# A decoder layer on one core: the up projection as seven half-size block products

## The chip, the cores and the metric

The kernel runs on one core of a Trainium2 chip. The metric is the device time of one execution in microseconds (us). The kernel before takes 798.82 us, the median of three runs (798.44 to 799.29).

## The reference

One layer of a hybrid decoder, for one sequence of 512 tokens of width 1024, in float32. The first half mixes tokens (a state-space group and a forgetting-attention group, side by side) and ends in an output projection that is added to the residual. The second half, which the change is about, is a gated MLP with a short convolution:

```python
x = x + (mixed @ w_out[layer].astype(mixed.dtype)).astype(x.dtype)
hf = rms_norm(x, norm_ffn_w[layer])
x = x + conv_gated_mlp(hf, w_up[layer], ffn_conv_w[layer], ffn_conv_b[layer], w_down[layer]).astype(x.dtype)
...
def conv_gated_mlp(x, w_up, conv_w, conv_b, w_down):
    h = x @ w_up.astype(x.dtype)                    # 512 x 1024 by 1024 x 5632
    h = causal_depthwise_conv(h, conv_w, conv_b)    # width 3, along the tokens
    gate, val = jnp.split(h, 2, axis=-1)            # 2816 columns each
    return (jax.nn.silu(gate) * val) @ w_down.astype(x.dtype)
```

## The kernel before, in words

**Arithmetic.** Every large matrix product is made of three matmuls in a reduced float32 format (`mm3`, line 88): each operand is split into a high part, a rounded copy that ScalarE makes, and a low part, the rest, which VectorE subtracts; high x high, high x low and low x high are summed in PSUM. So each block of weights (128 x 1024 numbers, 512 KB) is loaded by a DMA from SyncE's queue into a tile `wraw`, and split into `wh` and `wl` by one operation of ScalarE (line 84) and one of VectorE (line 85); three buffers of each turn round.

**Order.** The program is written in the order of the work, and a scheduler then orders the instructions of each engine beforehand by modelled times and priorities (`urgent()` raises a block's priority); on the chip each engine then takes its instructions in that fixed order. PSUM has eight banks of 128 x 512 numbers: three in the pool `pg`, four in `pm`, one in `po`.

**End of the mixer.** Projections of the attention heads are interleaved with pieces of the output projection (`fillers`, line 670; `a1` is a half of the second state-space group, `o0` to `o2` the first attention groups). The last piece, `out_proj((7,), mf[6:8])` (line 696), goes half of the output columns by half, and within each over the four blocks of 128 tokens. Each result is added to the residual `x2` by VectorE (line 258).

**Into the MLP.** GpSimd multiplies `x2` with the norm's weight (line 709), TensorE transposes the result (`hT`, line 712), and ScalarE and VectorE split it into `hh` and `hl`. The norm itself, a factor for each token, is not applied here: `second_norm` (line 792) sums the squares, takes the power on GpSimd (line 103) and spreads the factors over the partitions with a matmul (`rbc`, line 124) into `R2`.

**Up projection.** For each of 44 tiles of 128 output features `up_proj` (line 773) makes 8 x 3 matmuls of 512 columns (tokens) into one bank; the first tile is cut into two halves of 256 columns, 48 matmuls. `gated(j)` (line 805) multiplies the bank with `R2` (VectorE, line 811), makes the convolution with one operation of ScalarE (line 814) and two of VectorE (line 816), and applies SiLU to the gate (line 821). GpSimd forms gate x value and the sums S1 to S4 that the next step needs (lines 826 to 840).

**Down projection.** It is a block product already made of seven half-size products instead of eight (`PRODUCTS`, line 860), in tiles Y, X and Z. Its weights come in six units for each product; sums of weight blocks are formed in tiles `T` by DMAs of GpSimd's queue that add while they write (`gather`, line 758), after plain loads (`fresh`, line 755). The results are added to `x2` and stored.

Lines of the profile that the prediction uses: 84 and 85 (weight splits), 91 (all `mm3` matmuls), 103 (power on GpSimd), 124 (`rbc`), 258 (residual), 466 (a normalisation with two factors, in the mixer), 618 (a copy out of PSUM), 759 (issue of an adding DMA), 796 (squares), 811 to 829 (`gated`).

Of the kernel before, what the change touches and what calls it, by code (L numbers as in the profile page):

```python
# [8 lines left out]
F32 = mybir.dt.float32  # L9
# [29 lines left out]
def tile_hybrid_layer(  # L39
# [25 lines left out]
    pg = ctx.enter_context(tc.tile_pool(name="pg", bufs=3, space=PSUM))  # L65
    pm = ctx.enter_context(tc.tile_pool(name="pm", bufs=4, space=PSUM))
    po = ctx.enter_context(tc.tile_pool(name="po", bufs=1, space=PSUM))
# [20 lines left out]
    def mm3(o, ah, al, bh, bl, start, stop, grouped=True, keep=False):  # L88
        kw = {} if grouped else {"skip_group_check": True}
        for n, (a, b) in enumerate(((ah, bh), (ah, bl), (al, bh))):  # L90
            ins = pe.matmul(o, a, b, start=start and n == 0, stop=stop and n == 2, **kw)  # L91
            if keep:
                tc.keep_in_program_order(ins)

    def bank(name="g"):
        return pg.tile([P, 512], F32, tag="g", name=name)

    def mbank(name="m"):
        return pm.tile([P, 512], F32, tag="m", name=name)
# [241 lines left out]
    def ssd_proj(g):  # L341
# [6 lines left out]
        def to_tokens(j, src):  # L348
            t = po.tile([P, 512], F32, tag="o", name="xT")
# [255 lines left out]
    def fox_values(pair, turned, v):  # L605
        o = po.tile([P, 512], F32, tag="o", name="o")
# [9 lines left out]
        mh = pf.tile([P, SEQ], F32R, tag="mfh", name="mfh", bufs=2)  # L616
        ml = pf.tile([P, SEQ], F32R, tag="mfl", name="mfl", bufs=2)
# [7 lines left out]
    early = {8: b0, 10: feature_tile(second), 0: feature_tile(third, po.tile([P, 512], F32, tag="o", name="j0"))}  # L625
# [18 lines left out]
    pss_ctx.close()  # L644
    pf_ctx = ExitStack()
# [25 lines left out]

    def fill(name):
        if name[0] == "a":
# [22 lines left out]
    out_proj((7,), mf[6:8])  # L696

    hh = pxt.tile([P, NK, SEQ], F32R, tag="xh", name="hh")
    hl = pxt.tile([P, NK, SEQ], F32R, tag="xl", name="hl")
    nw = pf.tile([P, 1280], F32, tag="prob", name="nw", bufs=4)[:, :D]  # L700
    nc.sync.dma_start(nw, norm_ffn_w.to_broadcast([P, D]))
    for half in range(2):
        c = slice(half * 512, (half + 1) * 512)
        ks = slice(half * 4, half * 4 + 4)
        for tb in range(NTB):
            s = slice(tb * P, (tb + 1) * P)
            with urgent():
                xw = pf.tile([P, 512], F32, tag="pt1" if tb % 2 else "pt2", name="xw", bufs=3)
                (dve if (half, tb) == (1, 3) else pool).tensor_tensor(out=xw, in0=x2[:, tb, c], in1=nw[:, c], op=ALU.mult)
                t = mbank("hT")  # L710
                for j in range(4):
                    pe.transpose(t[:, j * P : (j + 1) * P], xw[:, j * P : (j + 1) * P], ident)
                tv = t.rearrange("p (j f) -> p j f", j=4)
                act.copy(hh[:, ks, s], tv)
                dve.tensor_sub(hl[:, ks, s], tv, raw(hh[:, ks, s]))
    pf_ctx.close()
    actx.close()

    pb = ctx.enter_context(tc.tile_pool(name="pb", bufs=1, reuse_waits="tile"))
    NH = NFF // 2  # L720
    HT = SEQ // 2
    N1, N2 = slice(0, 512), slice(512, 1024)

    def operand(slot=None):
        if slot is None:
            hl_ = [pb.tile([P, NH, HT], F32R, tag=t, name=t, bufs=2) for t in ("oh", "ol")]
            return hl_[0], hl_[1]
        pair_ = [pxt.tile([P, NK, SEQ], F32R, tag=t, name="o" + t) for t in ("xh", "xl")]
        return tuple(
            t.rearrange("p a b -> p (a b)")[:, 0 : NH * HT].rearrange("p (a b) -> p a b", b=HT) for t in pair_  # L730
        )

    a11, a12 = operand(), operand()
    a22 = pb.tile([P, NH, HT], F32, tag="a22", name="a22")
    S1, S2, S3, S4 = [pb.tile([P, NH, HT], F32, tag="S%d" % n, name="sum%d" % n) for n in (1, 2, 3, 4)]
    r2 = pb.tile([P, NTB], F32, tag="r2", name="r2")
    ss = pb.tile([P, NTB], F32, tag="ss", name="ss")
    UNITS = [(k, min(k + 2, NH)) for k in range(0, NH, 2)]
    B11, B12, B21, B22 = 0, 1, 2, 3
# [3 lines left out]

    raws = [0]

    def load_unit(q, u):
        where = wp if raws[0] % 5 < 3 else pb
        raws[0] += 1
        rw = where.tile([P, 1024], F32, tag="wraw", name="wraw", bufs=3 if where is wp else 2)
        nc.sync.dma_start(rw[:, 0 : (UNITS[u][1] - UNITS[u][0]) * 512], part(q, u))  # L750
        return rw
# [8 lines left out]

    def split_unit(u, src):
# [3 lines left out]
        act.copy(h[:, :n], src[:, :n])  # L765
        dve.tensor_tensor(out=l[:, :n], in0=src[:, :n], in1=raw(h[:, :n]), op=ALU.subtract)  # L766
        return h, l

    pu_ctx = ExitStack()
    pu = pu_ctx.enter_context(tc.tile_pool(name="pu", bufs=1, reuse_waits="tile"))  # L770
    R2 = pu.tile([P, SEQ], F32, tag="R2", name="R2")

    def up_proj(fs, cuts, between=None):
        ws = [load_split(wup[f], four=False) for f in fs]
        os = [bank("up") for _ in fs]
        w = SEQ // cuts
        for cut in range(cuts):
            s = slice(cut * w, (cut + 1) * w)
            for o, (h, l) in zip(os, ws):
                for k in range(NK):  # L780
                    ks = slice(k * P, (k + 1) * P)
                    pin = between is not None and k == NK // 2
                    if pin:
                        between()
                    mm3(
                        o[:, s], h[:, ks], l[:, ks], hh[:, k, s], hl[:, k, s], k == 0 and cut == 0, k == NK - 1,
                        grouped=cuts == 1, keep=pin,
                    )
        return os


    def second_norm():
        with urgent():
            for tb in range(NTB):
                junk = pb.tile([P, D], F32, tag="junk", name="junk", bufs=2)
                act.activation(junk, x2[:, tb, :], AF.Square, accum_out=ss[:, tb : tb + 1])
            token_scale(r2, R2, ss, pu)

    early = up_proj((0,), 2) + up_proj((NFF,), 1, between=second_norm)
# [5 lines left out]
    def gated(j):  # L805
        both = []
        for part in range(2):
            f = part * NFF + j
            o = early[part] if j == 0 else up_proj((f,), 1)[0]
            xp = pu.tile([P, SEQ], F32, tag="up", name="up", bufs=3)  # L810
            dve.tensor_mul(xp, o, R2)  # L811
            a = pu.tile([P, SEQ], F32, tag="ua", name="ua", bufs=5)
            cw = C_FCW + 3 * f
            act.activation(a, xp, AF.Identity, scale=pc[:, cw + 2 : cw + 3], bias=pc[:, C_FCB + f : C_FCB + f + 1])
            for s in range(1, 3):
# [210 lines left out]
```

## Time and profile before

| What | Value |
|---|---|
| Median of three runs | 798.82 us |
| Lowest and highest | 798.44 and 799.29 us |
| Span of the profiled execution | 799.4 us |
| TensorE (PE), weight loads (PEld) busy | 791.7, 645.6 us |
| VectorE (DVE), ScalarE (ACT), GpSimd (POOL) busy | 566.8, 428.7, 223.9 us |
| Granted TensorE clock over the span | 0.998 |
| Moved from and to HBM | 91.56 MB read, 2.20 MB written |
| End of the last down product to the end of the span | 794.6 to 799.4 us |

A busy time is the time in which at least one instruction of the engine ran; weight loads run beside matmuls. In a row of a group stand the line of the kernel, the engine, the operation, the tiles (out<-in), the shapes and the count, then busy time in us and mean of one in ns, then the idle time of the engine just before these instructions and what ended it. In a row of the chain or the timeline the first two numbers are start and duration in us. In a row of the windows each engine has its busy time and its count of instructions; the last three numbers are TensorE's clock, the mean busy share of the 16 DMA engines and GB/s.

### The profile page before, as it was taken

What the parts mean: (1) busy time and instruction counts of PE and PEld (TensorE: products, weight loads), DVE (VectorE), ACT (ScalarE), POOL (GpSimd) and SP (SyncE); (2) the same over time, 40 slices, a digit from 0 to 9 for tenths busy, and PEclk for the clock granted to TensorE, in tenths of its full rate; (3) what the DMA queues carried; (4) which work ended last, traced back from release to release, by engine and by line L of the source; (5) the groups of instructions that cost most, each with busy time, mean ns of one, the idle gap of its engine ahead of it and who ended that gap; (6) DMA issues with size and microseconds to landing.
All of it is one profiled execution on the core that took longest, in us unless ns stands there. A gap on an engine that the chain in (4) does not pass through costs nothing.

```text
span 799.4 us, 10603 instructions
## 1 busy us (share of the span) xinstructions
PE 791.7 (99%) x3789; PEld 645.6 (81%) x3789; DVE 566.8 (71%) x891; ACT 428.7 (54%) x779; POOL 223.9 (28%) x260
## 2 busy tenths in 40 slices
PE   8999999999999999999999999999999999999997
PEld 6888887877887877887877888888888888888886
DVE  4797997688567576597874677766766766778744
ACT  6556646552479477775752563444443444556531
POOL 0003231433233362243200434233333223233120
PEclk9999999999999999999999999999999999999999
DMA  9524322431244234252231463223223223299992
GB/s 325 179 80 138 130 80 80 146 131 53 80 159 132 54 130 133 68 161 89 84 100 54 134 183 106 92 92 106 93 91 106 98 87 106 91 247 190 219 189 91
DMA packets 31254, 98.12 MB, mean 123 GB/s; under 512 B 3873, under 2 KB 4961, under 8 KB 31201
## 3 DMA queue, kind: packets, MB, share of 16 engines
q1 hardware_dynamic: 26192, 81.71, 30.6%
q0 software_dynamic: 4576, 15.21, 10.1%
q8 instruction: 30, 0.49, 0.2%
q10 hardware_dynamic: 432, 0.52, 0.2%
q14 instruction: 24, 0.19, 0.1%
HBM read 91.56 MB, written 2.20 MB: 117 GB/s over the span
## 4 chain that ended last, share of the span: by engine, by line
PE 98%; DMA 1%; DVE 0%; SPq 0%; ACT 0%; DVEq 0%; issue 0%
PE up L91 30%; PE pw L91 22%; PE po L91 11%; PE g L91 7%; PE Y L91 5%; PE X L91 4%; PE Z L91 4%; PE o L610 2%; PE pT L600 2%; PE yd L436 2%; PE j L91 1%; PE S L577 1%; PE S L578 1%; PE qkT L527 1%; PE yo L442 1%; DMA xr<-in_xT_dram 1%
## 5 line engine op out<-in xcount | busy, mean ns | idle before, releaser
L84 ACT CAST wh<-wraw 128x1024 fp32r<-128x1024 f32 x103 | 108.1, 1050 | 109.0 <-PE up L91 75.2
L85 DVE TENSOR_TENSOR wl<-wraw,wh 128x1024 fp32r<-128x1024 f32 x103 | 132.0, 1282 | 26.2 <-ACT wh L84 23.9
L91 PE MATMUL up<-hh,wh 128*128 128x512 f32 (+1 forms) x360 | 138.9, 386 | 0.0
L91 PE MATMUL up<-hh,wl 128*128 128x512 f32 (+1 forms) x360 | 138.5, 385 | 0.0
L91 PE MATMUL up<-hl,wh 128*128 128x512 f32 (+1 forms) x360 | 138.5, 385 | 0.0
L91 PE MATMUL pw<-wh,xh 128*128 128x512 f32 x256 | 102.5, 402 | 0.0
L91 PE MATMUL pw<-wl,xh 128*128 128x512 f32 x256 | 101.8, 398 | 0.0
L91 PE MATMUL pw<-wh,xl 128*128 128x512 f32 x256 | 101.2, 397 | 0.0
L91 PEld LDWEIGHTS up<-hh,wh 128*128 128x128 f32 x360 | 67.6, 188 | 13.7 <-issue 0.2
L91 PEld LDWEIGHTS up<-hl,wh 128*128 128x128 f32 x360 | 67.6, 188 | 13.6 <-issue 0.2
L91 PEld LDWEIGHTS up<-hh,wl 128*128 128x128 f32 x360 | 67.6, 188 | 13.3
L811 DVE TENSOR_TENSOR up<-up,R 128x512 f32<-128x512 f32 x44 | 30.3, 691 | 58.6 <-PE up L91 58.6
L816 DVE SCALAR_TENSOR_TENSOR ua<-up,pc,ua 128x511 f32<-128x511 f32 (+1 forms) x88 | 66.8, 763 | 1.3
L91 PEld LDWEIGHTS pw<-wh,xl 128*128 128x128 f32 x256 | 48.1, 188 | 9.9 <-issue 0.5
L91 PEld LDWEIGHTS pw<-wl,xh 128*128 128x128 f32 x256 | 48.2, 188 | 9.6 <-issue 0.7
L91 PEld LDWEIGHTS pw<-wh,xh 128*128 128x128 f32 x256 | 48.1, 188 | 9.5 <-issue 0.5
L765 ACT CAST wh<-T 128x1024 fp32r<-128x1024 f32 (+1 forms) x30 | 29.3, 976 | 36.9 <-PE Z L91 15.3
L579 DVE CUSTOM_DVE_ANT_0 prob<-S,prob 128x128 f32<-128x128 f32 (+1 forms) x64 | 30.3, 487 | 24.7 <-PE S L578 24.4
L766 DVE TENSOR_TENSOR wl<-T,wh 128x1024 fp32r<-128x1024 f32 (+1 forms) x30 | 33.8, 1134 | 19.2 <-ACT wh L765 18.8
L583 ACT ACTIVATE prob<-prob,nm 128x128 f32<-128x128 f32 (+1 forms) x64 | 35.8, 560 | 21.1 <-DVE nm L579 20.4
L258 DVE TENSOR_TENSOR x<-po,x 128x512 f32<-128x512 f32 x48 | 32.6, 686 | 13.1 <-PE po L91 12.9
L826 POOL TENSOR_TENSOR ua<-ua 128x512 f32<-128x512 f32 x11 | 15.0, 1363 | 91.0 <-DVE ua L816 91.0
(238 smaller groups left out, 1691.9 us busy)
## 6 DMA issues: line engine op xcount, KB each, us to landing
wraw<-in_wup_dram SPq DMA_DIRECT2D x44, 512.0 KB, 3.3
T<-in_wdown_dram POOLq DMA_DIRECT2D x20, 512.0 KB, 7.1
wraw<-in_wqk_dram SPq DMA_DIRECT2D x16, 512.0 KB, 3.3
wraw<-in_wout_dram SPq DMA_DIRECT2D x16, 512.0 KB, 3.3
wraw<-in_wxbc_dram SPq DMA_DIRECT2D x11, 512.0 KB, 6.2
wraw<-in_wdown_dram SPq DMA_DIRECT2D x10, 512.0 KB, 3.6
T<-in_wdown_dram SPq DMA_DIRECT2D x10, 512.0 KB, 5.3
wraw<-in_wz_dram SPq DMA_DIRECT2D x8, 512.0 KB, 3.3
```

Source lines behind the costliest of these rows:

```text
L84: act.copy(h, r)
L85: dve.tensor_tensor(out=l, in0=r, in1=raw(h), op=ALU.subtract)
L91: ins = pe.matmul(o, a, b, start=start and n == 0, stop=stop and n == 2, **kw)
L258: dve.tensor_add(dst, banks[tb], dst)
L436: pe.matmul(yd[:, h * HD : (h + 1) * HD], sc[:, h, :], xdt[:, h * HD : (h + 1) * HD], start=True, stop=True)
L579: dve.tensor_tensor_reduce(out=p, in0=sps[:, :n], in1=p, scale=-1.0, scalar=-NEG, op0=ALU.add, op1=ALU.min, accum_out=nm[:, qb : qb + 1],)
L583: act.activation(p, p, AF.Exp, scale=-1.0, bias=nm[:, qb : qb + 1], accum_out=sm[:, qb : qb + 1])
L600: pe.transpose(t[:, w : w + P], prob[:, o : o + P], ident)
L765: act.copy(h[:, :n], src[:, :n])
L766: dve.tensor_tensor(out=l[:, :n], in0=src[:, :n], in1=raw(h[:, :n]), op=ALU.subtract)
L811: dve.tensor_mul(xp, o, R2)
L816: dve.scalar_tensor_tensor(out=a[:, s:], in0=xp[:, : SEQ - s], scalar=pc[:, cw + 2 - s : cw + 3 - s], in1=a[:, s:], op0=ALU.mult, op1=ALU.add,
```

## The change

**Up projection.** The normalised input is cut into four blocks A (two halves of the tokens by two halves of the 1024 inner features), the weights into four blocks B (two halves of the inner features; gate and value columns). For each `q` of 11 the gate and value features of tiles `q` and `q + 11`, four output tiles, are made by seven products of one A-operand with one weight block (128 x 1024) each. A product is 2 tiles x 4 inner pieces x 3 matmuls of 256 columns. The operands are A11, A12, A22, S1 = A21 - A22, S2 = S1 - A11, A11 - A21 and A12 + S2, made once and split; the weight operands are B11, B21, B22 and the sums B11 + B12, B11 + B12 + B22, B11 + B12 + B21 + B22 and B22 + B12. These sums grow in place in the tiles `ta` and `tb`, by adding DMAs from GpSimd's queue after each split. Each group owns two pairs of banks, G and Z; a product that is used in several results is accumulated on in the same half of a bank, and what is needed in between is copied out by ScalarE (`keep`, three times) or joined in PSUM by VectorE (three times). Two groups fill all eight banks.

**Norm.** The norm of each block of 128 tokens is now applied to `x2` before the transposes (`up_tokens`), so `rbc` and the multiplication with `R2` go; the convolution reads PSUM directly.

**Output projection.** Its end goes token block by token block (`out_part`): for each block the rest of `a1` (blocks 2 and 3), then both halves of the last group, then `up_tokens` of that block; the last block's transposes stand behind one and a half products of the up projection. The first three units of the first down product stand among the last products of the up projection, and the order of splits is held by hand (`ordered`). Below, `n2`, `n3` and `n5` are left out: they have the form of `n0` and `n1`, each with a split of `ta` or `tb`, an adding DMA and a product into a half of Z or G; `low12` subtracts a kept half from Z.

```diff
+    for tb in range(NTB):
+        if tb > 1:
+            out_part(wa1[0], m1, 1, (tb,))
+        for half in range(2):
+            out_part(w7[half], mf[6:8], half, (tb,))
+        if tb < NTB - 1:
+            with urgent():
+                up_tokens(tb)
...
+    def up_tokens(tb):
+        half, i = tb // 2, tb % 2
+        xw = xws[half][:, i, :]
+        s = slice(i * P, (i + 1) * P)
+        act.activation(xw, x2[:, tb, :], AF.Square, accum_out=ss[:, tb : tb + 1])
+        rt = r2[:, tb : tb + 1]
+        rsqrt(rt, ss[:, tb : tb + 1], 1.0 / D, 1)
+        t = two_banks("Z", "hT")
+        for c in range(2):
+            cs = slice(c * 512, (c + 1) * 512)
+            dve.scalar_tensor_tensor(
+                out=xw[:, cs], in0=x2[:, tb, cs], scalar=rt, in1=nw[c], op0=ALU.mult, op1=ALU.mult
+            )
+            for j in range(4):
+                o = c * 512 + j * P
+                pe.transpose(t[:, c, j * P : (j + 1) * P], xw[:, o : o + P], ident)
...
+        if half == 0:
+            act.copy(oh[:, 0:2, :, s], tv)
+            dve.tensor_sub(ol[:, 0:2, :, s], tv, raw(oh[:, 0:2, :, s]))
+            act.copy(one[:, :, :, s], tv)
+        else:
+            act.copy(two[:, 1, :, s], tv[:, 1])
+            dve.tensor_sub(s1[:, :, s], tv[:, 0], two[:, 1, :, s])
+            h = act.copy(oh[:, 3, :, s], s1[:, :, s])
+            l = dve.tensor_sub(ol[:, 3, :, s], s1[:, :, s], raw(oh[:, 3, :, s]))
...
+    def split_up(r):
+        h = wp.tile([P, 1024], F32R, tag="wh", name="wh", bufs=3)
+        l = wp.tile([P, 1024], F32R, tag="wl", name="wl", bufs=3)
+        ordered(act.copy(h, r), lambda: dve.tensor_tensor(out=l, in0=r, in1=raw(h), op=SUB))
+        return h, l
...
+    def product(w, n, o, part, first=False):
+        h, l = w
+        ah, al = up_operand(n)
+        for p in range(2):
+            for k in range(4):
+                c = slice(p * 512 + k * P, p * 512 + (k + 1) * P)
+                ins = mm3(
+                    o[:, p, part], h[:, c], l[:, c], ah[:, k], al[:, k], first and k == 0, k == 3, grouped=False
+                )
...
+    def keep(src, name):
+        t = pu.tile([P, 2, HT], F32, tag="kept", name=name, bufs=4)
+        take(act.copy(t, src))
+        return t
...
+    def more(t, quarter, q):
+        last_more[0] = nc.gpsimd.dma_start(t, wup[quarter, q], accum_op=ALU.add)
+
+    def n0(q):
+        u = quads[q]
+        u.ta = ptt.tile([P, 1024], F32, tag="T", name="Ta", bufs=2)
+        nc.sync.dma_start(u.ta, wup[B11, q])
+        w = split_up(u.ta)
+        more(u.ta, B12, q)
+        u.G = two_banks("G", "G")
+        product(w, 0, u.G, H2, True)
+        with urgent():
+            u.y0 = keep(u.G[:, :, H2], "y0")
+
+    def n1(q):
+        u = quads[q]
+        r = wp.tile([P, 1024], F32, tag="wraw", name="wraw", bufs=3)
+        nc.sync.dma_start(r, wup[B21, q])
+        product(split_up(r), 1, u.G, H1)
+        with urgent():
+            take(None, dve.tensor_tensor(out=u.G[:, :, H1], in0=u.G[:, :, H1], in1=u.y0, op=ADD))
...
+    def n6(q):
+        u = quads[q]
+        product(split_up(u.tb), 5, u.G, H2)
+        with urgent():
+            take(None, dve.tensor_tensor(out=u.Z[:, :, H2], in0=u.z2, in1=u.G[:, :, H2], op=SUB))
+
+    def n4(q):
+        u = quads[q]
+        product(split_up(u.ta), 2, u.G, H2)
...
+    for q in range(2, NH - 2):
+        n0(q + 1)
+        n6(q)
+        n2(q + 1)
+        n4(q)
+        gated(q)
+        n1(q + 1)
+        n5(q + 1)
+        n3(q + 1)
+        low12(q + 1)
```

More of the change, by code (lines that the diff above doesn't have):

```diff
@@ L1 @@
[L1 removed]
+from contextlib import ExitStack, nullcontext
 import concourse.bass as bass
@@ new lines, in take @@
+    def take(on_act, on_dve=None):
+        taken[made[0] - 1] = (on_act, on_dve)
+    class Quad:
+        pass
+    quads = [Quad() for _ in range(NH)]
+    H1, H2 = slice(0, HT), slice(HT, SEQ)
+    halfway = [None]
+    def product(w, n, o, part, first=False):
[7 more added lines that the diff above has]
+                )
+            if p == 0:
+                halfway[0] = ins
@@ new lines, in n3, with n5, low12 @@
+    def n3(q):
+        u = quads[q]
+        w = split_up(u.ta)
+        more(u.ta, B21, q)
+        product(w, 4, u.G, H2)
+        with urgent():
+            u.y3 = keep(u.G[:, :, H2], "y3")
+    def n5(q):
+        u = quads[q]
+        u.tb = wp.tile([P, 1024], F32, tag="wraw", name="Tb", bufs=3)
+        nc.sync.dma_start(u.tb, wup[B22, q])
+        w = split_up(u.tb)
+        more(u.tb, B12, q)
+        product(w, 6, u.Z, H1)
+    def low12(q):
+        u = quads[q]
+        with urgent():
+            dve.tensor_tensor(out=u.Z[:, :, H1], in0=u.Z[:, :, H1], in1=u.y3, op=SUB)
@@ L764, in split_unit @@
         l = wp.tile([P, 1024], F32R, tag="wl", name="wl", bufs=3)
-        act.copy(h[:, :n], src[:, :n])
-        dve.tensor_tensor(out=l[:, :n], in0=src[:, :n], in1=raw(h[:, :n]), op=ALU.subtract)
+        hs, ls = h[:, :n], l[:, :n]
+        ordered(act.copy(hs, src[:, :n]), lambda: dve.tensor_tensor(out=ls, in0=src[:, :n], in1=raw(hs), op=SUB))
         return h, l
[L769 to L799, printed above, removed]
     def split_into(o, src, lo, hi):
@@ L803, in split_into @@
         dve.tensor_sub(o[1][:, lo:hi, :], src[:, lo:hi, :], raw(o[0][:, lo:hi, :]))
[L805 to L815, printed above, removed]
-                dve.scalar_tensor_tensor(
-                    out=a[:, s:], in0=xp[:, : SEQ - s], scalar=pc[:, cw + 2 - s : cw + 3 - s], in1=a[:, s:],
-                    op0=ALU.mult, op1=ALU.add,
-                )
-            both.append(a)
-        act.activation(both[0], both[0], AF.Silu)
-        return both
@@ L883, in tile_hybrid_layer @@
         if nxt is not None:
-            ops.append(operand(1 if n % 3 == 1 else None))
-        tiles = [bank("X") for _ in range(2)] if tiles is None else tiles
+            ops.append(operand(n + 1))
+        tiles = halves("G", "X") if tiles is None else tiles
         lhs = ops[n]
```

328 lines of the change are left out of this document (234 added, 94 removed).

## The prediction

> **What bounds the kernel now.** I read the page first, for the shares of the engines and the chain that ended last, then the waits of TensorE.
>
> ```profile
> span 799.4 us, 10603 instructions
> PE 791.7 (99%) x3789; PEld 645.6 (81%) x3789; DVE 566.8 (71%) x891; ACT 428.7 (54%) x779; POOL 223.9 (28%) x260
> PE 98%; DMA 1%; DVE 0%; SPq 0%; ACT 0%; DVEq 0%; issue 0%
> PE up L91 30%; PE pw L91 22%; PE po L91 11%; PE g L91 7%; PE Y L91 5%; PE X L91 4%; PE Z L91 4%; PE o L610 2%; PE pT L600 2%; PE yd L436 2%; PE j L91 1%; PE S L577 1%; PE S L578 1%; PE qkT L527 1%; PE yo L442 1%; DMA xr<-in_xT_dram 1%
> ```
> ```profile
> PE g L196 <- ACT xh L162: 1.5, 1, 1.5
> PE g L188 <- DVE mhalf L111: 1.0, 1, 1.0
> PE g L200 <- DVE xl L163: 0.2, 1, 0.2
> ```
>
> TensorE is the chain, and its only waits, 2.7 us, lie at the very start. So the time moves with the work given to TensorE, as long as nothing new makes it wait. The span is 0.6 us above the median of the three runs (798.82); the sum below is made on the span and 0.6 is taken off at its end.
>
> A matmul's recorded duration is no measure, since matmuls overlap: what counts is the distance of their starts. The chain of waits gives it for 512 columns, the timeline of the first up tile, which is cut in two, for 256 columns (35 rows stand from the first to the last of this fence, all of 256 columns).
>
> ```profile
> 462.91 0.86 PE rbc L124 x2
> 463.77 225.80 PE up L91 x996
> ```
> ```profile
> 455.13 0.28 PE L91 MATMUL up<-hl,wh 128*128 128x256 f32 x1
> ...
> 459.20 0.28 PE L91 MATMUL up<-hh,wl 128*128 128x256 f32 x1
> ```
> ```profile
> L91 PE MATMUL up<-hh,wh 128*128 128x512 f32 x344 | 134.3, 390 | 0.0
> L91 PEld LDWEIGHTS up<-hh,wl 128*128 128x128 f32 x360 | 67.6, 188 | 13.3
> L91 PE MATMUL up<-hh,wh 128*128 128x256 f32 x16 | 4.6, 288 | 0.0
> ```
>
> With 512 columns a matmul takes 225.80 / 996 = 226.7 ns; with 256 it takes 4.07 us / 34 gaps = 119.7 ns. The weight load of 188 ns is longer than that, but 34 gaps in a row at 119.7 ns show that loads overlap one another too. Half the columns cost 53%, not 50%: 107.0 ns for 256 columns, and 12.7 ns that each matmul pays whatever its size.
>
> **The change: matmuls.** The three groups of `up` matmuls hold 3 x (344 + 16) = 1080: 1032 x 226.7 ns + 48 x 119.7 ns = 239.7 us, the 30% of the chain. After it there are 11 groups of weights, each with 7 products of 2 x 4 x 3 = 24 matmuls of 256 columns: 1848 x 119.7 ns = 221.2 us. That is 18.5 us less: an eighth of the columns less saves 28.2 us, and 768 more matmuls give 9.8 us of it back at 12.7 ns each. The broadcast of the second norm through TensorE (rbc, 0.86 us) goes as well. The 32 transposes and the matmuls of the output projection stay, as do the seven products of the down projection, in another order. Without any new wait the span becomes 799.4 - 18.5 - 0.9 = 780.0 us.
>
> The Trainium skill (TensorE: Matmul & The Clock Gate, "Back-to-back issue gap") gives N / 2.4 + 2.5 ns for a warm matmul, 109 ns at 256 columns and 216 ns at 512; here both rows lie 11 ns above it. By that rule of the Trainium skill the halving would be nearly free and the saving an estimated 26 us; the measured 119.7 ns decide.
>
> **The other engines in the up stage.** A group of four output tiles took 96 x 226.7 ns = 21.8 us; now it has 168 x 119.7 ns = 20.1 us.
>
> ```profile
> L85 DVE TENSOR_TENSOR wl<-wraw,wh 128x1024 fp32r<-128x1024 f32 x38 | 49.1, 1293 | 7.4 <-ACT wh L84 7.4
> L84 ACT CAST wh<-wraw 128x1024 fp32r<-128x1024 f32 x38 | 40.0, 1054 | 71.1 <-PE up L91 71.1
> L814 ACT ACTIVATE ua<-up,pc 128x512 f32<-128x512 f32 x39 | 31.7, 813 | 0.0
> L816 DVE SCALAR_TENSOR_TENSOR ua<-up,pc,ua 128x511 f32<-128x511 f32 x40 | 30.7, 768 | 0.0
> L811 DVE TENSOR_TENSOR up<-up,R 128x512 f32<-128x512 f32 x39 | 27.0, 691 | 54.1 <-PE up L91 54.1
> L821 ACT ACTIVATE ua<-ua 128x512 f32<-128x512 f32 x21 | 13.3, 632 | 45.8 <-DVE ua L816 45.8
> L829 DVE TENSOR_TENSOR ol<-ua,oh 128x256 fp32r<-128x256 f32 x10 | 9.6, 960 | 0.0
> L839 DVE TENSOR_TENSOR ol<-ua,oh 128x256 fp32r<-128x256 f32 x10 | 4.7, 473 | 0.0
> L828 ACT CAST oh<-ua 128x256 fp32r<-128x256 f32 x10 | 4.0, 400 | 0.0
> ```
> ```profile
> L618 ACT CAST mfh<-o 128x512 fp32r<-128x512 f32 x8 | 4.7, 586 | 9.6 <-PE o L610 9.3 <-PE po L91 0.3
> L759 POOL DMA_DIRECT2D T<-in_wdown_dram x24 | 21.0, 874 | 57.2 <-DVE wl L766 34.6 <-issue 9.1 <-DMA T<-in_wdown_dram 6.5
> L466 DVE SCALAR_TENSOR_TENSOR y<-y,ss,nwb 128x512 f32<-128x512 f32 x8 | 8.6, 1070 | 3.9 <-POOL ss L103 3.8
> L103 POOL TENSOR_TENSOR ss<-ss,mhalf 128x1 f32<-128x1 f32 x8 | 6.2, 776 | 22.8 <-DVE ss L102 22.8
> L796 ACT ACTIVATE junk<-x 128x1024 f32<-128x1024 f32 x4 | 4.2, 1051 | 0.0
> L826 POOL TENSOR_TENSOR ua<-ua 128x512 f32<-128x512 f32 x11 | 15.0, 1363 | 91.0 <-DVE ua L816 91.0
> ```
> ```profile
> core 0: us, PE busy (x) PEld busy (x) DVE busy (x) ACT busy (x) POOL busy (x), PEclk, DMA share, GB/s
> 100.00:120.00 20.00, 20.00 (x108) 16.36 (x107) 19.55 (x25) 9.21 (x23) 7.26 (x6) 1.00 0.23 80
> 470.00:680.00 210.00, 210.00 (x928) 173.90 (x927) 146.99 (x179) 91.57 (x130) 66.22 (x60) 1.00 0.31 100
> 690.00:705.00 15.00, 15.00 (x68) 12.43 (x67) 13.60 (x17) 10.16 (x17) 4.83 (x4) 1.00 0.55 165
> ```
>
> VectorE now: seven weight splits instead of four (7 x 1.293 = 9.05); the four multiplications by the norm go, and three half-bank joins come, each on 512 elements read from PSUM like L811 (3 x 0.69 = 2.07; below that only if a write into PSUM is cheaper, which no row shows); eight convolution steps (8 x 0.768 = 6.14), which now read PSUM themselves; one split of the gated product (0.47 to 0.96). That is 17.7 to 18.2 us of 20.1, 88 to 91%, against 70% in the window from 470 to 680. ScalarE: 7 x 1.054 + 3 copies out of PSUM of 0.586 + 4 x 0.813 + 2 x 0.632 + 0.40 = 14.1 us, 70%. GpSimd: its present 66.22 us over 9.65 groups, 6.9 us, and four issues of 0.874: 10.4 us, 52%. None is over its time. The window from 100 to 120 shows VectorE at 98% and the one from 690 to 705 at 91%, and TensorE is busy in all of both: a full VectorE alone costs nothing, but one that is full and stands in a chain that TensorE needs may.
>
> **The sums of weights.** Four of the seven weight blocks are now sums that an accumulating DMA from GpSimd's queue adds into the tile after it was split, so the tile `ta` runs through load, split, add, split, add, split, add, split.
>
> ```profile
> q0 software_dynamic: 3168, 10.49, 55.2%
> q1 hardware_dynamic: 2880, 8.39, 23.5%
> T<-in_wdown_dram POOLq DMA_DIRECT2D x18, 512.0 KB, 7.1
> T<-in_wdown_dram SPq DMA_DIRECT2D x8, 512.0 KB, 6.4
> ```
> ```profile
> DMA to landing us min/median/max: 3.5/6.9/10.2
> wraw<-in_wup_dram SPq DMA_DIRECT2D x44, 512.0 KB, 3.3
> ```
>
> These are the DMAs of the last 105 us (690 to 795), where the down projection does the same, and the row of all transfers into T. There the accumulating queue moved 20 blocks of 0.52 MB in 55.2% of 105 us, 2.9 us of all 16 engines each; a plain block cost 24.7 / 16 = 1.5 us. A group now needs four and three: 16.2 us of 20.1, 81%, against 31%. The chain of one `ta` is 4 x (1.054 + 1.293) = 9.4 us of splits, 3 x 7.1 = 21.3 us of adds and 3.3 to 6.4 us of load: 34.0 to 37.1 us. Two such tiles alternate, so it may take two groups, 40.2 us. The slack of 3 to 6 us has to pay for some eight hand-overs, each behind whatever stands in the queues of ScalarE, VectorE and GpSimd (0.6 to 1.3 us an operation). I expect part of it to be lost: 0.45 us of TensorE time a group, 5.0 us in all. The ends are 0 and, with every add at 10.2 us, (46.4 - 40.2) / 2 = 3.1 us a group, 34 us.
>
> **The hand-over into the up projection.** The chain of waits shows what eight transposes take:
>
> ```profile
> 444.87 0.87 PE hT L712 x8
> ```
>
> Before, the norm was applied after the matmul, so no matmul waited for it. Now each block of 128 tokens goes through add to x2 (0.69, as L811), squares (1.05), GpSimd's power (0.78), two normalisations of the form of L466 (2.14), eight transposes (0.87) and then copies and subtractions out of PSUM (about 2 x 0.59 + 2 x 0.69): some 8.1 us. The last block has four products (11.5 us) before the first that needs it, but its transposes stand in TensorE's queue after one and a half products (4.3 us), and they need the first 4.7 us of the chain. Blocks 0 and 1 must be done before the first product, with only the projections of blocks 2 and 3 (5.4 to 10.9 us) as cover and VectorE busy with weight splits beside them. I take 2.5 us lost; the ends are 0 and about 8, all of one such chain.
>
> **The end of the up stage.** The last gated tile is needed by the last of the down product's six units; 36 matmuls (8.2 us) stand before, and its own chain is 0.81 + 2 x 0.77 + 0.63 + 1.36 (L826) + 0.40 + 0.96 = 5.7 us. I take 0; if the other three convolutions go first (4.6 us more), 2.
>
> **Sum.** 780.0 + 5.0 + 2.5 + 0 = 787.5 us of span, less 0.6: **786.9 us**. The likeliest case's own range is 779.4 (no wait at all) to 795.
>
> **Rivals.** (1) The weight sums bind, and the kernel becomes slower. For it: 81% of the DMA engines and a chain with 3 to 6 us of slack. Against it: 7.1 us is a median of a stage that kept the DMA engines as busy, and TensorE waited for none of them there (but they had a whole product of 15 us between). It decides from about 9.1 us an add, where (9.4 + 27.3 + 6.4 - 40.2) / 2 = 1.5 us a group eats 17 us; at 10.2 it ends at 780.0 + 2.5 + 34 - 0.6 = 816 us. (2) The half banks bind: a product must not accumulate on a half before ScalarE or VectorE has read it, with one product (2.9 us) between, and PSUM is full with two groups, so the gate's four convolution steps (3.1 us) must end within three products beside three splits and two joins (5.3 us): 8.4 of 8.6 us. At 1.5 us a group lost the gain is gone: 799 us. The Trainium skill (PSUM — Partial Sum Buffer, "PSUM bank collisions raise a hardware error") asks for guarding a bank as a whole, so a product on one half would wait for a reader of the other half too; no run here shows such a wait yet, and it would add to this rival. (3) The norm's chains queue up on VectorE at the hand-over and cost 8 us more: 795 us. (4) The 12.7 ns are not paid in long runs of the small form: 1848 x 12.7 ns = 23 us less, 763 us; the 34 gaps in a row speak against it. The rule of the Trainium skill above (TensorE: Matmul & The Clock Gate) would have 2.5 ns in place of the 12.7.
>
> **Chances.** Forecast 0.60, (1) 0.16, (2) 0.12, (3) 0.10, (4) 0.02. A run of this kernel can tell 0.2%, 1.6 us, from no change. The forecast and (4) are faster; (3) is faster for 0.08 and the same for 0.02; (2) lies around the old time and is split 0.03, 0.05, 0.04; (1) is slower. Faster 0.73, same 0.07, slower 0.20. The range from 779 to 803 leaves out (4) and nearly all of (1).
>
> **What would show it.** Right: matmuls into G and Z with starts 119.7 ns apart, 221 us of them, no rbc; VectorE near 90% and DMA near 0.8 in the stage; a few us of TensorE waits, most of them for `wh` or `wl` made from a sum. Rival 1 shows as waits of the splits for the DMA into T, rival 2 as matmuls waiting for joins or convolutions, rival 3 as a gap ahead of the first products. The prediction is wrong if TensorE waits over 17 us in all, or if the starts lie apart by anything but 120 ns.

## The result and the profile after

| | before | after |
|---|---|---|
| Median of 4 runs | 798.79 us | 810.55 us |
| Lowest and highest | 798.44 and 799.29 us | 807.92 and 813.62 us |
| Ratio, 95% interval | | 1.0146 (1.0121 to 1.0172) |
| Span of the profiled execution | 799.4 us | 809.3 us |

The change makes the kernel slower by 1.5%; the forecast was 786.9 us. Below are the head of the page of the kernel after, its chain by engine, and the row of its adding DMAs with the median from issue to landing.

```profile
span 809.3 us, 12324 instructions
PE 782.3 (97%) x4555; PEld 669.5 (83%) x4555; DVE 619.3 (77%) x922; ACT 479.1 (59%) x834; POOL 254.3 (31%) x300
PE 70%; DVE 11%; DMA 8%; issue 6%; ACT 2%; POOL 2%; POOLq 0%; DVEq 0%; ACTq 0%
Ta<-in_wup_dram POOLq DMA_DIRECT2D x33, 512.0 KB, 5.5
```

Before, 98% of the chain was TensorE; now 70% is, and a quarter runs over VectorE, DMAs and the issue of instructions. The largest waits of TensorE in the kernel after (us in all, times, longest) tell what for; all its rows come to 21.4 us, more than the 17 us that the prediction named as a sign of being wrong:

```profile
PE G L95 <- DVE wl L823: 4.4, 8, 1.4
PE G L95 <- ACT wh L823: 3.4, 3, 1.8
PE X L95 <- DVE wl L1045: 3.0, 2, 2.5
PE G L95 <- DVE Z L912: 2.0, 1, 2.0
PE G L95 <- DVE ua L923: 1.5, 1, 1.5
PE G L95 <- DVE x L692: 1.3, 1, 1.3
```

Line 823 holds the splits of the up weights, line 1045 those of the down weights, 912 is a join of two halves, 923 the convolution, 692 the add to the residual ahead of the norm. Where nothing waits, the pace is the one that was worked out: the chain that ended last has 24 matmuls in 2.88 us, 120.0 ns each.

```profile
671.39 2.88 PE Z L95 x24
674.27 2.88 PE G L95 x24
```

The windows of the kernel after show where TensorE stands still.

```profile
core 0: us, PE busy (x) PEld busy (x) DVE busy (x) ACT busy (x) POOL busy (x), PEclk, DMA share, GB/s
447.00:470.00 23.00, 20.29 (x166) 19.92 (x167) 20.41 (x24) 16.55 (x23) 4.95 (x6) 1.00 0.77 153
470.00:500.00 30.00, 25.19 (x189) 24.18 (x188) 19.01 (x23) 14.17 (x18) 5.37 (x6) 0.94 0.70 165
500.00:530.00 30.00, 25.47 (x202) 24.27 (x201) 19.61 (x24) 16.25 (x22) 13.71 (x16) 1.00 0.54 103
560.00:600.00 40.00, 39.63 (x329) 39.24 (x328) 36.55 (x37) 24.34 (x32) 17.39 (x18) 1.00 0.77 174
600.00:640.00 40.00, 38.29 (x316) 37.76 (x315) 37.94 (x38) 24.88 (x33) 19.64 (x20) 1.00 0.78 176
700.00:720.00 20.00, 16.93 (x73) 13.13 (x72) 18.88 (x27) 15.32 (x26) 11.25 (x9) 1.00 0.83 244
```

In the first 83 us of the up stage it stands for 12 us, in the middle for 0.4 to 1.7 us of 40, and for 3 us where the down projection begins. In the middle VectorE is at 91 to 95%, a little above the forecast of 88 to 91%, and the DMA engines are at 0.77 to 0.78, a little below the forecast of 81%.

A finer clock of the stage is the moment at which ScalarE splits the first gated tile of each of the eleven groups (line 939, one row each in the timeline). The summary row of that line holds the first and the last of them; the table has all, for three kernels, the second and third of which are experiments below.

```profile
L939 ACT CAST oh<-ua x11: 405/409/410, 499.3 to 705.6; 128x256 fp32r<-128x256 f32 x11
```

| us from one to the next group | start to 1st | 1-2 | 2-3 | 3-4 | 4-5 | 5-6 | 6-7 | 7-8 | 8-9 | 9-10 | 10-11 |
|---|---|---|---|---|---|---|---|---|---|---|---|
| after | 51.5 | 16.5 | 24.5 | 20.6 | 20.6 | 21.0 | 21.5 | 20.7 | 20.1 | 25.0 | 15.6 |
| plain weight blocks | 46.2 | 14.2 | 19.8 | 20.1 | 20.1 | 20.1 | 20.1 | 20.1 | 20.1 | 25.3 | 15.6 |
| without GpSimd's sums | 51.1 | 15.2 | 24.7 | 20.1 | 20.1 | 20.1 | 20.1 | 20.1 | 21.0 | 24.1 | 15.6 |

The start is the first product (447.8, 448.4 and 448.4 us). In the steady part a group takes 20.1 us where nothing holds it, the 20.1 us of the prediction, and 20.1 to 21.5 us after. The big losses lie in the first three columns. Four later runs whose up stage is that of the change have 49.6 to 51.2 us in the first column, so its 51.5 is good to about 2 us.

### The profile page after: what moved, and what is told of

Read it like the earlier page. It is cut to its first block, busy times and chain, and to the rows that moved or that the text cites. A ratio compares the mean times of both kernels' runs of the same rounds, so it can differ in the third digit from the quotient of the medians.

```text
span 809.3 us, 12324 instructions
## 1 busy us (share of the span) xinstructions
PE 782.3 (97%) x4555; PEld 669.5 (83%) x4555; DVE 619.3 (77%) x922; ACT 479.1 (59%) x834; POOL 254.3 (31%) x300
## 4 chain that ended last, share of the span: by engine, by line
PE 70%; DVE 11%; DMA 8%; issue 6%; ACT 2%; POOL 2%; POOLq 0%; DVEq 0%; ACTq 0%
PE pw L95 22%; PE po L95 10%; PE g L95 7%; DVE wl L823 6%; DMA Ta<-in_wup_dram 6%; PE Z L95 5%; PE Y L95 4%; PE G L95 4%; PE X L95 3%; PE o L618 2%; PE pT L608 2%; DMA Tb<-in_wup_dram 2%; DVE ua L923 2%; PE yd L444 2%; ACT wh L823 2%
## 5 line engine op out<-in xcount | busy, mean ns | idle before, releaser
L89 DVE TENSOR_TENSOR wl<-wraw,wh 128x1024 fp32r<-128x1024 f32 x59 | 75.0, 1271 | 14.6 <-ACT wh L88 14.4
L95 PE MATMUL G<-uh,wh 128*128 128x256 f32 x264 | 75.9, 287 | 5.6 <-DVE Z L912 2.0
L95 PE MATMUL G<-uh,wl 128*128 128x256 f32 x264 | 75.4, 286 | 0.0
L95 PE MATMUL G<-ul,wh 128*128 128x256 f32 x264 | 75.4, 286 | 0.0
L823 ACT CAST wh<-Ta 128x1024 fp32r<-128x1024 f32 x44 | 45.9, 1048 | 36.9 <-DMA Ta<-in_wup_dram 29.3
L823 DVE TENSOR_TENSOR wl<-Ta,wh 128x1024 fp32r<-128x1024 f32 x44 | 53.5, 1221 | 16.8 <-ACT wh L823 16.7
L823 DVE TENSOR_TENSOR wl<-Tb,wh 128x1024 fp32r<-128x1024 f32 x22 | 49.7, 2264 | 14.2 <-ACT wh L823 14.0
L95 PEld LDWEIGHTS G<-uh,wh 128*128 128x128 f32 x264 | 51.3, 194 | 6.5 <-ACT y L851 2.6
L95 PE MATMUL G<-sh,wl 128*128 128x256 f32 x176 | 50.6, 287 | 4.4 <-DVE wl L823 4.4
L95 PE MATMUL G<-sh,wh 128*128 128x256 f32 x176 | 49.8, 283 | 3.4 <-ACT wh L823 3.4
L95 PEld LDWEIGHTS G<-ul,wh 128*128 128x128 f32 x264 | 51.4, 195 | 0.0
L95 PEld LDWEIGHTS G<-uh,wl 128*128 128x128 f32 x264 | 51.4, 195 | 0.0
L95 PE MATMUL G<-sl,wh 128*128 128x256 f32 x176 | 49.6, 282 | 0.0
```

The source lines that it names most:

```text
L89: dve.tensor_tensor(out=l, in0=r, in1=raw(h), op=ALU.subtract)
L823: ordered(act.copy(h, r), lambda: dve.tensor_tensor(out=l, in0=r, in1=raw(h), op=SUB))
```

## The experiments

Theory: the weight sums (load, split, add, split, each sum in the tile of the one before it) cost the time. Rivals: GpSimd's sums of gated products hold VectorE; the operands made from sums of the input come late; the norm at the hand-over. The times below are medians of 4 runs (5 for the three edits together); before ran beside each at 798.8 to 800.1 us, the change's own median is 810.55 us.

### Plain weight blocks

```diff
-        more(u.ta, B12, q)
...
-        w = split_up(u.ta)
-        more(u.ta, B22, q)
+        w = split_up(plain(B12, q))
...
```

> Leaves out the sums of weight blocks: each of the seven products takes one plain block, loaded by SyncE's queue into a tile of its own turn, so there is no adding DMA and no chain of split and add (the results are not the layer's). The number of splits, products, joins and bytes loaded stays. Theory A (the chain of split, add, split makes TensorE wait): 12 us or more below the 810.6 us of the change, with the waits between 466 and 530 us mostly gone. Theory B (GpSimd's sums of the gated product hold up VectorE's splits): 0 to 2 us below, the long splits of 4 to 5 us stay. Theory C (norm and operand sums at the hand-over fill VectorE): 0 to 4 us below, the waits between 447 and 500 us stay.

795.52 us, ratio 0.9950 (0.9934 to 0.9967): 15.0 us less than the change. The second row of the table shows where: 5.3 + 2.3 + 4.7 us in the filling of the first three groups, 3.9 us in the next six. Three windows of this run:

```profile
470.00:500.00 30.00, 28.27 (x230) 27.51 (x229) 23.78 (x27) 18.48 (x23) 6.43 (x6) 1.00 0.49 159
500.00:530.00 30.00, 29.55 (x247) 29.36 (x246) 27.26 (x31) 19.13 (x27) 11.57 (x10) 1.00 0.56 194
560.00:600.00 40.00, 40.00 (x336) 40.00 (x335) 34.34 (x38) 25.81 (x34) 14.95 (x12) 1.00 0.53 182
```

Not one wait is left in the middle, with VectorE still at 86%. So the sums of weights are the main cause. The run also takes load off the DMA engines (0.53 busy in the middle instead of 0.77), but in the change the splits of the up stage wait for the tiles of the sums, and no row has them wait for a plain block in `wraw`:

```profile
ACT wh L823 <- DMA Ta<-in_wup_dram: 29.3, 15, 4.8
ACT wh L823 <- DMA Tb<-in_wup_dram: 5.5, 4, 4.4
```

Even so the kernel is only 0.5% faster than before, not 2.4%: some 14 us lie elsewhere.

### Without GpSimd's sums, and both

```diff
-        pool.tensor_tensor(out=S3[:, j, :], in0=g1, in1=g2, op=SUB)
...
-        pool.tensor_tensor(out=S1[:, j, :], in0=g2, in1=k2, op=SUB)
-        pool.tensor_tensor(out=S2[:, j, :], in0=S1[:, j, :], in1=g1, op=SUB)
-        pool.tensor_tensor(out=S4[:, j, :], in0=k1, in1=S2[:, j, :], op=ADD)
```

> Leaves out GpSimd's S1 to S4 in every group (the down projection takes halves of the gated product in their place); all else is as in the change. Theory B: the splits of Tb that take 4.3 to 5.0 us fall to 1.2 us, and the waits of TensorE from 530 to 700 us (about 4 us in all) go: 805 to 807 us. Theory A: no change beyond 2 us, the waits for splits of sums stay. Theory C: no change.

> Both left out at once: the sums of weight blocks (plain loads in their place) and GpSimd's S1 to S4. Alone they gave 15.0 and 6.0 us. If they are two causes that only add up: 789.5 us. If GpSimd's hold on VectorE matters only because the chain of adds has no slack (theory: one cause, two links): 793 to 796 us, as with plain weights alone.

Without the sums 804.55 us, 6.0 us less; with plain weights as well 794.23 us, 1.3 us less than plain weights alone. The two don't add up, so GpSimd's sums cost time mostly by way of the weight chain: the third row of the table has its steady groups back at 20.1 us, but for one. How this may come about, the timelines of GpSimd and of VectorE in the kernel after show (start, duration):

```profile
537.72 1.62 POOL L937 TENSOR_TENSOR ua<-ua 128x512 f32<-128x512 f32 x1
539.00 1.59 POOL L942 TENSOR_TENSOR KK<-ua 128x512 f32<-128x512 f32 x1
540.25 1.02 POOL L941 TENSOR_TENSOR sum<-ua 128x256 f32<-128x256 f32 x1
540.95 1.02 POOL L944 TENSOR_TENSOR sum<-ua,KK 128x256 f32<-128x256 f32 x1
542.04 1.61 POOL L945 TENSOR_TENSOR sum<-sum,ua 128x256 f32<-128x256 f32 x1
```
```profile
538.11 4.95 DVE L823 TENSOR_TENSOR wl<-Tb,wh 128x1024 fp32r<-128x1024 f32 x1
```

A split that takes 1.23 us elsewhere takes 4.95 us beside five GpSimd operations in a row, two products and three sums. The splits of `Tb`, with the least, the median and the greatest duration in ns, in the kernel after, without GpSimd's sums, and with plain weights:

```profile
L823 DVE TENSOR_TENSOR wl<-Tb,wh x22: 1212/1226/4950, 469.1 to 683.9; 128x1024 fp32r<-128x1024 f32 x22
```
```profile
L823 DVE TENSOR_TENSOR wl<-Tb,wh x22: 1217/1226/3564, 469.6 to 679.2; 128x1024 fp32r<-128x1024 f32 x22
```
```profile
L823 DVE TENSOR_TENSOR wl<-Tb,wh x22: 1214/1226/1760, 469.5 to 668.7; 128x1024 fp32r<-128x1024 f32 x22
```

Without the sums one split in every steady group still takes 3.56 us, beside the two products; with them it takes up to 1.4 us more. With plain weights GpSimd does the same sums, but the splits fall at other times, and none of them takes more than 1.8 us. That the 1.4 us are what TensorE then waits for fits the traces, but no run changed them alone. The Trainium skill (SBUF — State Buffer, "Who interferes with whom") says that a VectorE instruction with two inputs in SBUF contends with a GpSimd instruction that reads SBUF; the 4.95 us agree.

### Without the sums of the input as operands

```diff
-        return (oh[:, n], ol[:, n]) if n < 4 else (sh[:, n - 4], sl[:, n - 4])
+        n = (0, 1, 0, 3, 3, 0, 1)[n]
+        return oh[:, n], ol[:, n]
...
-            make_operand(n)
+            pass
```

> Leaves out the three further operand sums and the split of A22 (some 9 us of VectorE and 8 us of ScalarE around 460 to 472 us): these products take operands that exist already. Theory C: the wait of 2 us at 466 us goes and those behind it shrink, 4 to 8 us below the change. Theory A: at most 2 us below, since the adds still have to land.

> Plain weight blocks (no adding DMA in the up stage) and no sums of the input's blocks as operands: leaves out both. Theory: the first stop that plain weights left, 1.7 us at 467 us, and one of 1.0 at 489, come from the operands made from sums of the input; they go, and the time falls from 795.5 by 2 to 3 us to 793. Rival: the input operands are not what stops TensorE; the stops stay and the longer hand-over that the run without operand sums showed (2.6 us for 1.5) comes back: 796 to 800 us.

815.24 us alone, 4.7 us more; with plain weights 795.54 us, no change. A stop of 1.7 us at 467 us (the distance of two starts less the usual one; the rows of waits, counted from the end of the matmul before, give up to 0.2 us less), in the first product with S2, which plain weights had left, is gone in the second run: the trace names ScalarE's split of the weights there, and ScalarE makes the operands ahead of it. But the wait ahead of the first product is 2.5 us in that run, where it was 1.3:

```profile
PE G L95 <- DVE x L692: 2.5, 1, 2.5
```

and TensorE's clock fell in both. In the run with the weight sums:

```profile
447.00:470.00 23.00, 21.15 (x165) 21.18 (x166) 14.14 (x17) 10.79 (x16) 4.75 (x7) 0.93 0.65 138
470.00:500.00 30.00, 24.61 (x179) 23.57 (x178) 16.94 (x20) 12.36 (x15) 3.30 (x4) 0.90 0.72 172
```

The change has 1.00 and 0.94 there: by an estimate from these rows, 0.07 x 23 + 0.04 x 30 = 2.8 us of the 4.7. The operands are refuted as a main cause.

### The last block's norm ahead of its output projection

```diff
+        with urgent():
+            up_tokens(tb)
         for half in range(2):
             out_part(w7[half], mf[6:8], half, (tb,))
-        if tb < NTB - 1:
-            with urgent():
-                up_tokens(tb)
...
-    with urgent(), tc.issue_after(halfway[0].ins):
-        up_tokens(NTB - 1)
```

> The norm, transposes and splits of each token block go ahead of its last output projection group, so the chain of the norm is covered by that group's matmuls (leaves the last attention group out of the normalised input). Theory C: the gap of 1.3 us ahead of the first product goes and the first 80 us of the up stage get 3 to 6 us shorter. Theory A: at most 2 us below.

Each block is normalised and transposed before the last group's part is added to it. 821.70 us, 11 us more, a miss: the last block's chain now stands ahead of the first product, with one piece of the projection as cover. A new row among the waits, and the window of that place:

```profile
PE hT L778 <- DVE xw L773: 2.5, 1, 2.5
447.00:470.00 23.00, 18.68 (x135) 17.98 (x135) 19.43 (x21) 11.67 (x16) 4.28 (x5) 0.85 0.50 112
```

It shows that the cover which the change gives to the last block (one and a half products) is worth having, not what the hand-over costs.

### Weight sums made beforehand in HBM

Copies of weight blocks in HBM are added to while the mixer runs, and the up stage loads finished sums: all four of a group, two of four, and two of four spread thin, with a copy at every second weight load.

```diff
+            d = dp.tile([P, 1040], F32, tag="ws%d_%d" % (key, q), name="ws%d_%d" % (key, q))[:, :1024]
+            nc.sync.dma_start(d, base(q))
+            nc.gpsimd.dma_start(d, wup[add, q], accum_op=ALU.add)
...
```

> The whole layer, with all four weight sums of each group made ahead in HBM, by plain copies and adding DMAs that are spread over the mixer's loads, and loaded as plain blocks in the up stage. If the chain of adds is the cause and the mixer has DMA time to spare: about 795 us, as with plain weights, and faster than before. If 44 copies and 44 adds more (some 190 us of all DMA engines over 400 us) hold up the mixer's loads or GpSimd's queue: the gain of the up stage is given back ahead of it, 800 to 820 us.

> The whole layer, with two of the four sums (the first of the chain, and the one of tile Tb) made ahead in HBM; two adds stay in the chain of Ta. Half the extra DMA work in the mixer. If it is the first, shortest link of the chain that makes TensorE wait: 795 to 798 us. If any add in the chain does: 800 to 806 us.

> As in the run with two sums of each group made ahead in HBM (B11+B12 and B22+B12), but one plain copy with every second weight load of the mixer from the 6th on, and its adding DMA only at the load after it, so that GpSimd's queue never stands waiting for the copy. Theory: the 12 us that the mixer lost in that run came from the density of the added transfers (DMA busy 0.7 to 0.97 up to 200 us) and from GpSimd's blocked queue; spread over 50 to 350 us the mixer loses under 2 us, the up stage starts at 447 to 449 us and the whole takes 798 to 802 us, since the up and down stages keep their 344 us. Rival: 22 copies and 22 adds cost the mixer the same wherever they stand; the up stage starts after 457 us and the time is 809 to 813 us.

854.04, 812.45 and 812.19 us. In the up stage it does what the theory says. With two sums of four, spread thin, the first three columns of the table are 47.0, 15.7 and 21.3 us, with all four 48.4, 13.5 and 20.2, and the six after them 20.1 to 20.2 in both. The first three add up to 92.5 us in the change, 84.0 with two sums made beforehand, 82.1 with four and 80.2 with plain weights: the loss of the filling goes with the adds. But the mixer pays. The windows from 100 to 200 us, of the kernel before and then of the three in this order:

```profile
100.00:200.00 100.00, 100.00 (x494) 80.58 (x493) 79.96 (x109) 48.60 (x113) 35.07 (x27) 1.00 0.29 98
```
```profile
100.00:200.00 100.00, 88.52 (x424) 70.20 (x424) 65.24 (x93) 46.48 (x109) 39.96 (x37) 0.97 0.78 215
```
```profile
100.00:200.00 100.00, 94.72 (x453) 75.42 (x454) 72.31 (x98) 49.55 (x116) 43.03 (x38) 0.97 0.75 213
```
```profile
100.00:200.00 100.00, 97.54 (x474) 77.92 (x474) 78.85 (x108) 47.83 (x111) 39.75 (x33) 0.98 0.58 169
```

Spread thin, the loss goes from 0 to 200 us into all of 0 to 300 us, and the up stage begins at 461 us as with two dense sums. That density was the reason is refuted. The other half of that theory, that GpSimd's queue is held, was not: in this run too it stood waiting for the copies, 118.6 us in all, and right behind some of these waits comes the work that TensorE then waits for in the mixer, the power of a normalisation and the issue of a small DMA (below the wait in all, and one place on GpSimd ahead of a stop of TensorE at 221 us):

```profile
POOL ws L86 <- DMA ws<-in_wup_dram: 118.6, 18, 14.2
```
```profile
216.72 0.85 POOL L86 DMA_DIRECT2D ws<-in_wup_dram  x1 [14.18 <-DMA ws<-in_wup_dram]
217.33 0.85 POOL L135 TENSOR_TENSOR ss<-ss,mhalf 128x1 f32<-128x1 f32 x1
```

How much of the loss comes this way stays open, since no run had the adds without that wait.

### The start in another order, and all three edits

```diff
     n2(1)
     later(4)
-    n3(0)
     later(6)
     n5(0)
+    n5(1)
+    n3(0)
     low12(0)
+    later(5)
     n3(1)
-    later(5)
+    low12(1)
     n6(0)
-    n5(1)
-    low12(1)
     later(2)
```

> The change with another order of the first two groups: the products of plain B22 stand between the first product with a sum of weights and the next, as they do in all later groups, so that split, add and split of a tile have three products between them and not one. Theory: the stops of TensorE between 463 and 525 us (about 12 us in all) come from the chain of split, add and split without a product to cover it; half of them go, and the time falls by 4 to 7 us to 804 to 807 us. Rival: they come from the operands of the input (S2, A12+S2), which are made at the same time; then the first of these products waits as long as before or longer, and the time is 809 to 812 us.

> The three edits of this group of runs together: two of four sums of each group made ahead in HBM, spread thin over the mixer; sums of the down projection issued one product later; plain B22 ahead of the second sum in the first two groups. If each removes what its theory says, and the gains of the first and the third overlap by half: 800 - 3 - 2 = 795 us (793 to 798), which is below the kernel before. If the mixer pays for the copies: 803 to 808 us.

The second run adds two thin sums in HBM and the later down sums (next part). 819.17 and 819.07 us: 8.6 and 8.5 us more than the change, a miss. In the second the mixer pays again (first product at 457.7 us). In the first, the first stop stayed, 1.8 us at 466 us, and one of 2.1 us followed at 469, as the rival had it. Then new ones came:

```profile
PE G L95 <- DVE ua L923: 3.6, 1, 3.6
PE Z L95 <- ACT wh L823: 2.5, 1, 2.5
```

a product waited 3.6 us for a convolution to give a half bank free. The order of the first groups is bound by PSUM too, so a better order of the filling was not found.

### The start of the down projection

```diff
-        if n == 0 and u < 2:
+        if n == 0:
             return
+        if n == 1 and u < 4:
+            fresh(B11, u + 2)
+            gather(B12, u + 2)
...
```

> The change with one edit: the plain loads and adding DMAs into T for units 3 to 6 of the down projection are issued one product later, each behind the weight load of a unit of X, and not in one burst of four. Theory: X's waits at 710 to 722 us (2.5 + 0.8 us) come from that burst, which stands ahead of X's weight loads in SyncE's queue (3.6 us of issue) and shares the DMA engines with them; they go, and the time falls by 3 us to 807 to 808 us. Rival: X's waits come from the splits on ScalarE and VectorE, which make S1's operand beside the weights; they stay, and the time is 810 to 811 us, or longer by 1 to 3 us if Z's weight sums now come late.

810.61 us, with X's wait of 2.4 us in place. The order in SyncE's queue was still the old one (four loads of T at 708.3 us, then X's weights at 712.1), so this didn't test the loads. Next, the operand splits: those of KK's first half for the second product (left out), then S1's, then S1's with plain weights and no sums of the input.

```diff
-                for v in (2 * u - 6, 2 * u - 5):
-                    split_into(ops[1], nxt, *UNITS[v])
```
```diff
-            elif n > 0 and nxt is not None:
+            elif n > 1 and nxt is not None:
```

> Leaves out the split of the second down product's operand, which the change moved from the up loop into the first down product (that product takes the first one's operand again). If VectorE's work there is what holds the start of the down projection (TensorE idle for some 4 us between 700 and 722 us): those waits go, 3 to 5 us below the change's 810.6. If the waits come from the weight splits as such: no change beyond 1 us.

> The change without the splits of S1 during the down projection's second product (the third product takes the second one's operand): leaves out part of the computation. Theory: X's waits at 715 to 720 us (2.6 + 0.8 us) come from VectorE and ScalarE, where pieces of S1 are split ahead of the weights that X needs; they go, and the time falls by 3 us to 807 to 808 us. Rival: they come from X's weight loads, which stand behind four plain loads into T in SyncE's queue (the run with later sums of the down projection left them there); they stay, and the time is 810 to 811 us.

> Plain weight blocks, no operand sums, no splits of S1: all three left out. If these three are the causes of the waits that are left, the time is 789 to 791 us (795.5 - 2.5 - 3); the rest above the 780.0 us of the sum without waits is then the hand-over (1.5 us), the last 1.0 us and stops of half a microsecond. If it stays at 793 us or above, the stops at the start have another cause.

811.11, 811.87 and 795.89 us: no change in any. Without S1's splits those of a later operand stood at the same place on VectorE, so only leaving out all of them tells:

```diff
-            ops.append(operand(n + 1))
+            ops.append(ops[1] if n else operand(1))
...
-            elif n > 0 and nxt is not None:
-                split_into(ops[n + 1], nxt, lo, hi)
```

> The change without any split of the down projection's operands S1, S2, second half of KK, S4 and S3 (the third to seventh product take the second one's operand): leaves out these splits. In the run without S1's splits alone, those of S2 stood in the same place on VectorE, so it did not tell; now nothing stands there. Theory: X's waits at 715 to 720 us (2.6 + 0.8 us) come from these splits ahead of X's weights; they go, and the time falls by 3 us to 807 to 808 us. Rival: they come from X's weight loads behind the four loads into T; they stay, and the time is 810 to 811 us.

> Plain weight blocks, no operand sums in the up stage and no splits of the down projection's later operands: leaves out all three. If the splits are what X waits for: 792 us (795.5 - 3 to 3.5), with the wait at 699 us gone. If not: 795 to 796 us as in the two runs before.

805.10 and 790.67 us: 5.5 us less than the change, 4.9 us less than plain weights. From X's first matmul (705.1 us in the change) to the last one ahead of the final wait (800.4 us) the time fell from 95.3 to 91.1 us without the splits. In the timeline of VectorE in the kernel after (first fence) six pieces of a split, with an add among them, stand ahead of the weights (`wl`) for which X waits; the second fence is the window of the run without them.

```profile
712.77 2.43 DVE L1050 TENSOR_TENSOR ol<-sum,oh 128x512 fp32r<-128x512 f32 x3
715.12 0.68 DVE L1160 TENSOR_TENSOR x<-x,Y 128x512 f32<-128x512 f32 x1
715.72 1.62 DVE L1050 TENSOR_TENSOR ol<-sum,oh 128x512 fp32r<-128x512 f32 x3
717.26 1.21 DVE L1045 TENSOR_TENSOR wl<-wraw,wh 128x1024 fp32r<-128x1024 f32 x1
```
```profile
700.00:720.00 20.00, 18.86 (x80) 14.47 (x79) 13.78 (x17) 8.84 (x11) 11.90 (x10) 1.00 0.84 246
```

TensorE is busy for 18.86 us of 20 instead of 16.93, VectorE for 13.78 instead of 18.88, and SyncE's queue has the same order of loads as in the change. So it is the splits.

## Why the prediction was wrong, point by point

**The matmuls** were right: 120.0 ns in the trace for the 119.7 that were read, and 20.1 us a group without waits. The 12.7 ns that each matmul pays were paid, so rival 4 is out.

**The step that failed is "I expect part of it to be lost: 0.45 us of TensorE time a group, 5.0 us in all"**, the sums of weights. They cost 15.0 us. The steady part of it was near: the next six groups lost 3.9 us, 0.65 each. What the sum left out is the filling, 12.3 us in the first three columns of the table: it reasoned with two tiles in alternation over two groups, 40.2 us, and 3 to 6 us of slack, as if the groups overlapped from the start. The chain that ended last in the kernel after has adds on it there, and the steps between them are splits, GpSimd's work and issue:

```profile
505.43 5.41 DMA Ta<-in_wup_dram
515.41 7.61 DMA Ta<-in_wup_dram
525.76 5.54 DMA Ta<-in_wup_dram
```

That the adds cost this is shown (plain weights, and the sums made beforehand); why the filling suffers and the steady groups hardly do is argued only. In the first groups most successive sums of one tile have a single product between them (`n2` to `n3`, `n5` to `n6`), 5.8 us from start to start, and an add of 5.5 us with two splits of 1.05 and 1.22 us takes longer. But the run that widened this spacing was slower, by other stops, and in the later groups `n0` and `n2` lie as close, so this stays open.

**Rival 1** (the weight sums bind, slower) had the right place and sign and the wrong point of decision: it asked for adds of 9.1 us, and they took 5.5 us, less than the 7.1 us assumed.

**The steady loss** had a part that the prediction didn't have: without GpSimd's sums it is nearly gone, and beside GpSimd's products and sums VectorE's splits take up to 4.95 us. Counting VectorE at 88 to 91% with 1.29 us a split missed it.

**The end of the up stage, "I take 0"**, was 4 to 5 us. The reason was not the late gated tile, which was weighed and cost 0.6 us in the rows of waits, but the splits of the next operands on VectorE ahead of the weights for X, in a stretch where VectorE is 94% busy.

**The hand-over, 2.5 us**, was about right: the stop ahead of the first product is 1.5 us, and the first product with a sum of the input waits another 1.7 us with plain weights; the change moves both by a few tenths.

**Rival 2** (half banks) shows only in the filling: 2.8 us in four stops between 488 and 504 us with plain weights, which stay in the barest run, and the 3.6 us of the reordered start. In the change itself four such stops come to 5.6 us (the waits for lines 912, 923 and, twice, for a copy by ScalarE), so part of what the sums cost reaches TensorE by way of half banks that are freed late. **Rival 3**, 8 us at the hand-over, did not come.

The sum without waits was 780.0 us of span, and the barest run has 790.3. Of the change's 29.3 us above the sum, 15.0 are the weight sums, 4 to 5 the splits of the down projection, 3.2 the hand-over and the first operand, 2.8 the filling's half banks and 1.0 a last stop at 800 us; some 3 us, about as much as the runs differ among themselves, are not told apart.

## What to carry to other kernels

A saving that is worked out for the steady state must also pay for the filling, which here took most of what the sums cost: lay the chain of the first two or three rounds out by hand, with the cover that each step has there. In a chain with little slack, look for what else can slow its links (a neighbour that shares an engine's inputs) before taking a duration from a calm stage. And leaving out one piece of work proves nothing where an ordered queue puts the next piece in its place: look at the order that resulted.

## What the runs showed of the hardware

TensorE's clock fell to half here after short stops. After stops of 1.2, 0.9 and 2.2 us within 8 us the starts go from 0.12 to 0.21 us apart and stay so until 498.4 us, with a granted clock of 0.50 from 496 to 498 us; in the timeline of TensorE in the kernel after:

```profile
495.06 0.35 PE L95 MATMUL G<-uh,wh 128*128 128x256 f32 x1
495.21 0.42 PE L95 MATMUL G<-ul,wh 128*128 128x256 f32 x1
495.42 0.41 PE L95 MATMUL G<-uh,wl 128*128 128x256 f32 x1
495.63 0.41 PE L95 MATMUL G<-uh,wh 128*128 128x256 f32 x1
```

That costs some 1.5 us beside the stops themselves: 17 starts from 495.06 to 498.59 us, 3.53 us, where 120 ns each would be 2.04. The Trainium skill (TensorE: Matmul & The Clock Gate, "HAM oscillation — how this bites in real kernels") warns of idle gaps above about 3.4 us; here no single gap ahead of it was longer than 2.2 us, and the measurement decides. The length of one stop alone doesn't settle it: with plain weights and no operand sums a stop of 2.5 us ahead of the first product is followed by a granted clock of 0.50 from 449 to 452 us, while after X's stop of 2.5 us in the change the clock stays at 1.00.

And 22 copies and 22 adds of 512 KB, spread from 25 to 327 us over a mixer whose DMA engines are 0.3 to 0.4 busy after the first 50 us, went with a delay of the first product of the up stage by 13 us (447.8 to 460.7).
